# Attention scores drained two PSUM banks at a time, and every value product in three rounded passes

## The chip, the cores and the metric

The kernel runs on one core of one Trainium2 chip. The metric is the device time of one execution in microseconds (us); of several runs the median counts. A core has a matrix engine (TensorE, PE in the profile; its weight loads are PEld), a vector engine (VectorE, DVE), ScalarE (ACT), GpSimd (POOL) and SyncE (SP), which issues most of the DMAs here. Matrix results land in PSUM, which has 8 banks of 512 fp32 columns; VectorE and ScalarE read them from there.

## The reference, cut to what matters

The reference is one layer of a diffusion backbone over 2048 latent tokens with 256 context tokens, width 1024, all in fp32. One input projection feeds two head groups: gated linear attention, and differential softmax attention with 4 heads. Only the second is touched here:

```
s = einsum('bhqcd,bhkcd->bhcqk', q, k_all) * DIFF_DH ** -0.5     # c: two maps per head
p = softmax(s, axis=-1)
a = p[:, :, 0] - lam * p[:, :, 1]
o = einsum('bhqk,bhkd->bhqd', a, v_all)
```

There are 2304 keys (context and latent). `o` is normalised per head, joined with the other group's output, and goes through the output projection `w_out` with a gated residual; a SwiGLU feed-forward follows.

## The kernel before, in words

Precision comes from splitting. `split(hi, lo, src)` (L88) makes a rounded copy `hi` of a tile on ScalarE (L89, type float32r) and the rest `lo = src - hi` on VectorE (L86). `mm3` (L91 to L94) then makes a product in three passes, hi*hi, lo*hi and hi*lo (L92, L93, L94). A product of two fp32 tiles takes one call and no split; the profile shows it as two records.

The kernel runs in stages: input projections (stage 1), linear attention (stage 2), differential attention (stage 3), output projection (stage 4), feed-forward (stages 5 and 6). In stages 1 to 4 what TensorE does follows the order of the program; the other engines' instructions are put in order by the framework, by priority.

In stage 3, work is cut into 16 blocks, 4 heads times 4 groups of 4 query tiles (128 queries each). Two streams are interleaved on TensorE:

- `score_stream`. For each query tile and each map c there is a row of scores, 128 x 2304, made in five chunks (`CH`: four of 512 columns, one of 256). A chunk is two matmuls into one PSUM bank (L775, L776), with queries split into `qh` and `ql`. VectorE then drains it (L777): it copies the bank into the row `p` in SBUF and writes the chunk's maximum into `mx`. After the fifth chunk the maximum over `mx` is taken (L781) and ScalarE replaces the row by its exponential with the row's sum (L783). `combine` then scales the second map's row on VectorE (L807, two halves of 1152 columns) and GpSimd adds it to the first (L83). The chunks' banks come from the pool `s3ps` with `NS` = 4 buffers of one bank.
- `av_stream`. For each block and each of 18 key tiles it transposes four 128x128 pieces of `p` into one bank (L820), copies them out, and two steps later multiplies them with the value tile into the bank `o`. For key tiles whose number modulo 6 is in `VFP` = (0, 3), the copy is `at` (ScalarE, L823) and the product is one fp32 product (L843). For the others the copy is the split pair `ah` (ScalarE, L89) and `al` (VectorE, L86), and the product is `mm3`. At the end of a block `ot` and `on` are copied out and stored (L848 to L864).

There are 128 rows of scores, 640 chunks, and 288 value products, of which 96 in fp32. The PSUM use of stage 3 is 4 banks for chunks, 3 for transposes, 1 for `o`. Value tiles come from DRAM, written in stage 1 (`proj`): whole for the fp32 ones (`vf`), as `vh` and `vl` for the others; `load_v` fetches them in groups of six.

In stage 4, `prep(lt)` makes the operand of one token tile: it loads the attention's output into `mx`, squares it on ScalarE with `mh` as scratch (L985), scales it (L995), transposes `mx` in two halves (L1002) and splits it into `mh` and `ml`. `main(lt)` multiplies with the split `w_out` rows `wo`, in the orders `ORD0` and `ORD1`. The raw rows of `w_out` are loaded into staging tiles `wr` that are borrowed from other pools, and split during the last block of stage 3. Pools of a stage are stacked on one another in the order in which they are entered, so a tile of stage 4 lies over certain tiles of stage 3 and waits for just these to be released.

Of the kernel before, what the change touches and what calls it, by code (L numbers as in the profile page):

```python
# [11 lines left out]
F32 = mybir.dt.float32  # L12
F32R = mybir.dt.float32r
AF = mybir.ActivationFunctionType
ALU = mybir.AluOpType
AX = mybir.AxisListType
PSUM = bass.MemoryType.PSUM
DRAM = bass.MemoryType.DRAM

P = 128  # L20
# [12 lines left out]
NS, NTB, NO = 4, 3, 1  # L33
# [6 lines left out]
CD, LAG, LOOK = 4, 12, 2  # L40
MS = {mybir.EngineType.PE}
BKL = (3, 6, 9, 12)
PB, VFP = 6, (0, 3)
CSPLIT = ((2, 0, 1152), (2, 1152, 2304))
WPOOL = (0,)
VF = tuple(t for t in range(NK // P) if t % 6 in VFP)
VH = tuple(t for t in range(NK // P) if t not in VF)
# [4 lines left out]
def dit_block(ctx: ExitStack, tc: tile.TileContext, x, c, cx, c_ctx, w_mod, b_mod, norm1_g, w_in, gate_up,  # L52
              gate_bias, gla_g, qn_g, kn_g, lam_q, lam_k, diff_g, w_out, norm2_g, w_fi, w_fo,
              cosf, sinf, lmask, out, dbg=None):
    nc = tc.nc
    V, S, T, G = nc.vector, nc.scalar, nc.tensor, nc.gpsimd
# [13 lines left out]
    def dtile(name, shape, dt=F32):  # L70
        return dram.tile(list(shape), dt, name=name, tag=name)
# [16 lines left out]
    def split(hi, lo, src):  # L88
        return S.activation(hi, src, AF.Copy), sub(lo, src, f(hi))  # L89

    def mm3(ps, a, b, start, stop, **how):  # L91
# [36 lines left out]
    su_d = [(dtile(f"sf{t}", [64, 512]), dtile(f"ub{t}", [64, 512])) for t in range(NT)]  # L128
    q_d = [dtile(f"q{u}", [P, 4, SEQ], F32R) for u in "hl"]
    k_d = [dtile(f"k{u}", [P, 4, NK], F32R) for u in "hl"]  # L130
    v_d = {"f": dtile("vf", [P, len(VF), 512]), "h": dtile("vh", [P, len(VH), 512], F32R),
           "l": dtile("vl", [P, len(VH), 512], F32R)}
    md_d = [[dtile(f"md{h}_{t}", [P, P]) for t in range(NT)] for h in range(4)]
    x1_d = [dtile(f"x1_{t}", [P, D]) for t in range(NT)]
# [37 lines left out]
    with ExitStack() as st:  # L172
# [3 lines left out]
        st1 = st.enter_context(ExitStack())  # L176
# [12 lines left out]
        for t in range(2):  # L189
            xt = wk.tile([P, D], F32, name="xt", tag="xt")  # L190
# [514 lines left out]
    with ExitStack() as st:  # L705
        sm = st.enter_context(tc.tile_pool(name="s3m", bufs=6, reuse_waits="tile"))
# [4 lines left out]
        qp = st.enter_context(tc.tile_pool(name="s3q", bufs=2, reuse_waits="tile"))  # L711
        kp_ = st.enter_context(tc.tile_pool(name="s3k", bufs=3, reuse_waits="tile"))
        pb = st.enter_context(tc.tile_pool(name="s3pb", bufs=PB, reuse_waits="tile"))
        ps_s = st.enter_context(tc.tile_pool(name="s3ps", bufs=NS, space=PSUM, reuse_waits="tile"))
        ps_t = st.enter_context(tc.tile_pool(name="s3pt", bufs=NTB, space=PSUM, reuse_waits="tile"))
        ps_o = st.enter_context(tc.tile_pool(name="s3po", bufs=NO, space=PSUM, reuse_waits="tile"))
        NKT = NK // P
        CH = [(0, 512), (512, 512), (1024, 512), (1536, 512), (2048, 256)]
# [42 lines left out]
        def score_stream():  # L761
            later, ring = [], iter(range(64))
            for bi, (h, qb, i0, nq) in enumerate(blocks):
                as_[bi] = []
                for i in range(i0, i0 + nq):
                    qd = qs_[h, qb, i // 2]
                    qc = slice(i % 2 * P, (i % 2 + 1) * P)
                    pr = [(pa if next(ring) % (4 + PB) < 4 else pb).tile([P, NK], F32, name="p0", tag="p0"), sp.tile([P, NK], F32, name="p1", tag="p1")]
                    as_[bi].append(pr[0])
                    ls = []  # L770
                    for c_ in range(2):
                        mx = sm.tile([P, 5], F32, name="mx", tag="mx")
                        for j, (o0, n) in enumerate(CH):
                            ps = ps_s.tile([P, 512], F32, name="s", tag="s")
                            T.matmul(ps[:, 0:n], qd[0][c_][:, qc], ks_[h, c_][:, o0:o0 + n], start=True, stop=False)  # L775
                            T.matmul(ps[:, 0:n], qd[1][c_][:, qc], ks_[h, c_][:, o0:o0 + n], start=False, stop=True)  # L776
                            V.tensor_scalar(out=pr[c_][:, o0:o0 + n], in0=ps[:, 0:n], scalar1=1.0, scalar2=-3.0e38,  # L777
                                            op0=ALU.mult, op1=ALU.max, accum_out=mx[:, j:j + 1])
                            if j == len(CH) - 1:
                                nm = sm.tile([P, 1], F32, name="nm", tag="nm")  # L780
                                V.tensor_reduce(out=nm, in_=mx, axis=AX.X, op=ALU.max, negate=True)  # L781
                                l = l0all[:, qb * 4 + i, h:h + 1] if c_ == 0 else sm.tile([P, 1], F32, name="l1", tag="l1")
                                S.activation(pr[c_], pr[c_], AF.Exp, bias=nm, accum_out=l)  # L783
                                ls.append(l)
                                if c_ == 1:
                                    later.append([CD, combine(pr, ls, bi == len(blocks) - 1 and i >= i0 + nq - 2)])
                            for e in list(later):
                                e[0] -= 1
                                if e[0] < 0:
                                    e[1]()  # L790
                                    later.remove(e)
                            yield
            for e in later:
                e[1]()
# [72 lines left out]
        due, n = [], 0  # L867
# [26 lines left out]
    with ExitStack() as st:  # L894
# [16 lines left out]
        st1 = st.enter_context(ExitStack())  # L911
        xlp = rsk.enter_context(tc.tile_pool(name="s4xl", bufs=1, side="right", reuse_waits="tile"))
        gp = st1.enter_context(tc.tile_pool(name="s4gt", bufs=1, reuse_waits="tile"))
        htp = st1.enter_context(tc.tile_pool(name="s4ht", bufs=2, reuse_waits="tile"))
        wp = st1.enter_context(tc.tile_pool(name="s4w", bufs=1, reuse_waits="tile"))
        ph = st1.enter_context(tc.tile_pool(name="s4h", bufs=2, reuse_waits="tile"))
        ps_gm = st1.enter_context(tc.tile_pool(name="s4gm", bufs=1, space=PSUM, reuse_waits="tile"))
        ps_tp = st1.enter_context(tc.tile_pool(name="s4tp", bufs=3, space=PSUM, reuse_waits="tile"))
        ps_mm = st1.enter_context(tc.tile_pool(name="s4mm", bufs=4, space=PSUM, reuse_waits="tile"))
# [2 lines left out]
        xp = st1e.enter_context(tc.tile_pool(name="s4x", bufs=4, side="right", reuse_waits="tile"))  # L922
        xnp = st1e.enter_context(tc.tile_pool(name="s4n", bufs=2, side="right", reuse_waits="tile"))
        pp = st1e.enter_context(tc.tile_pool(name="s4p", bufs=2, reuse_waits="tile"))
# [4 lines left out]
        state = {}  # L929
        wo = {k: tuple(wp.tile([P, D], F32R, name=f"wo{u}_{k}") for u in "hl") for k in ORD1}  # L930
        for n, k in enumerate(ORD0):
            pool, tag = {3: (xnp, "xn"), 2: (xnp, "xn"), 1: (ph, "mh"), 0: (ph, "ml")}.get(k, (xp, "xt"))
            w = pool.tile([P, D], F32, name="wr", tag=tag)
            load(w, w_out[0, k * P:(k + 1) * P, :])
            with tc.high_priority(offset=tc.cur_priority - marks[3 + 2 * n]):
                split(*wo[k], w)
# [316 lines left out]
        with tc.manual_schedule(engines=MS):  # L1253
# [6 lines left out]
            for m, (n, i) in enumerate(flat):  # L1260
# [13 lines left out]
                ps = product(n, i)  # L1274
# [27 lines left out]
        with tc.manual_schedule(engines=MS):  # L1302
            for n, (dd, lt) in enumerate(pairs):
                js = slice(dd * 512, (dd + 1) * 512)
                ps = [ps6.tile([P, 512], F32, name="o", tag="o") for _ in range(2)]
# [73 lines left out]
```

## Time and profile before

| | |
|---|---|
| median of 3 runs | 3092.88 us (3092.88 to 3094.99) |
| the profiled execution: its time, its span | 3094.64 us, 3092.9 us |
| busy: PE, PEld, DVE | 3016.1 us (98%), 2483.7 us (80%), 2203.8 us (71%) |
| busy: ACT, POOL | 1423.5 us (46%), 463.8 us (15%) |
| granted TensorE clock, mean | 0.992 |
| the score drains (L777) | 640, 382.3 us busy |
| fp32 value products (L843) | 192 records, 922.2 to 1514.1 us |

Busy time is the union of an engine's instructions. Matmuls overlap in the pipeline, so a record is longer than the step from one matmul to the next; the same holds, less strongly, for VectorE. How long an instruction holds its engine is read from the timeline, as the step from its start to the next start where nothing was waited for. Shares over the whole span mix stages with different limits; the stretches of stage 3 are looked at by themselves.

### The profile page before, as it was taken

To read this page: it belongs to the slowest core of one execution; us is meant where nothing else is said; L and a number is where in the kernel's file an instruction comes from. 1 tells how busy PE (TensorE), PEld (TensorE's weight loads), DVE (VectorE), ACT (ScalarE), POOL (GpSimd) and SP (SyncE) were. 2 spreads that over 40 slices of the span, in tenths; PEclk is the share of its full clock that TensorE was granted. 3 is DMA by queue.
4 is the path that set the end of the run, shared out by engine and by line. 5 is a ranking of instruction groups with operands and counts; after the bars stand their busy time and mean duration, and the time that the engine had idled before them with its cause. 6 is when DMAs were issued, how large, how long until landed. Compare 5 with 4: busy or idle time off the path is not lost.

```text
span 3092.9 us, 41887 instructions
## 1 busy us (share of the span) xinstructions
PE 3016.1 (98%) x15124; PEld 2483.7 (80%) x15124; DVE 2203.8 (71%) x4788; ACT 1423.5 (46%) x2259; POOL 463.8 (15%) x290
## 2 busy tenths in 40 slices
PE   7999999999989999999999999999999999999999
PEld 4888888888867777777787788888788888888887
DVE  6887768888889999999787776666766666324232
ACT  5333366666657777777644433333433333113111
POOL 2111100000036555555111000000000000000000
PEclk9999999999999999999999999999999999999999
DMA  8876511121151313121445442222322225445342
GB/s 312 280 237 224 192 66 63 66 93 65 49 154 34 91 34 93 35 76 35 143 164 163 158 136 82 82 85 69 88 82 86 82 86 179 149 136 180 130 135 90
DMA packets 319121, 363.46 MB, mean 118 GB/s; under 512 B 25409, under 2 KB 256258, under 8 KB 312258
## 3 DMA queue, kind: packets, MB, share of 16 engines
q1 hardware_dynamic: 316322, 351.35, 36.2%
q0 software_dynamic: 2304, 8.39, 0.7%
q8 instruction: 119, 1.95, 0.3%
q10 hardware_dynamic: 288, 1.05, 0.1%
q14 instruction: 88, 0.72, 0.1%
HBM read 249.96 MB, written 110.76 MB: 117 GB/s over the span
## 4 chain that ended last, share of the span: by engine, by line
PE 63%; DVE 4%; issue 2%; DMA 1%; ACT 1%; POOL 1%; DVEq 0%; SPq 0%; ACTq 0%; POOLq 0%
PE p L93 9%; PE p L92 9%; PE p L94 9%; PE o L93 6%; PE o L94 6%; PE o L92 6%; PE s L775 4%; PE s L776 4%; PE t L820 4%; PE o L843 3%; PE mm L92 1%; PE mm L93 1%; PE mm L94 1%; POOL p L83 0%; DMA wo<-in_w_ffn_out 0%
## 5 line engine op out<-in xcount | busy, mean ns | idle before, releaser
L83 POOL TENSOR_TENSOR p<-p,p 128x1152 f32<-128x1152 f32 x124 | 354.8, 2882 | 283.5 <-DVE p L807 175.8
L777 DVE TENSOR_SCALAR_CACHE_REDUCE p<-s 128x512 f32<-128x512 f32 (+1 forms) x640 | 382.3, 632 | 13.2 <-PE s L776 9.2
L92 PE MATMUL mm<-wh,hh 128*128 128x512 f32 (+2 forms) x976 | 378.7, 388 | 0.0
L94 PE MATMUL mm<-wh,hl 128*128 128x512 f32 (+2 forms) x976 | 355.0, 364 | 1.1 <-DVE hl L86 1.1
L93 PE MATMUL mm<-wl,hh 128*128 128x512 f32 (+2 forms) x976 | 353.8, 363 | 0.0
L783 ACT ACTIVATE p<-p,nm 128x2304 f32<-128x2304 f32 x128 | 283.8, 2217 | 44.5 <-DVE nm L781 44.5
L775 PE MATMUL s<-k,qh 128*128 128x512 f32 (+1 forms) x640 | 276.4, 436 | 7.7 <-DVE p L777 6.9
L83 DVE TENSOR_TENSOR e<-p,e 128x512 f32<-128x512 f32 x220 | 152.1, 691 | 161.1 <-PE p L94 161.1
L92 PE MATMUL o<-wot,ah 128*128 128x512 f32 x682 | 265.4, 389 | 1.1 <-ACT wot L89 1.1
L93 PE MATMUL o<-wot,ah 128*128 128x512 f32 x682 | 265.4, 389 | 0.2 <-DVE wot L86 0.2
L94 PE MATMUL o<-wot,al 128*128 128x512 f32 x682 | 265.3, 389 | 0.0
L89 ACT ACTIVATE wh<-wi 128x512 fp32r<-128x512 f32 x172 | 108.4, 631 | 293.4 <-PE p L93 228.4
L776 PE MATMUL s<-k,ql 128*128 128x512 f32 (+1 forms) x640 | 235.6, 375 | 1.3 <-DMA ql<-ql 1.3
L89 ACT ACTIVATE ah<-ar 128x1408 fp32r<-128x1408 f32 x62 | 82.6, 1374 | 318.0 <-PE o L93 314.4
L94 PEld LDWEIGHTS mm<-wh,hl 128*128 128x128 f32 x976 | 184.8, 189 | 31.2 <-DVE hl L86 1.5
L92 PEld LDWEIGHTS mm<-wh,hh 128*128 128x128 f32 x976 | 185.9, 190 | 22.9 <-issue 0.7
L93 PEld LDWEIGHTS mm<-wl,hh 128*128 128x128 f32 x976 | 186.1, 191 | 21.4 <-issue 0.5
L86 DVE TENSOR_TENSOR al<-ar,ah 128x1408 fp32r<-128x1408 f32 x62 | 98.3, 1622 | 134.1 <-ACT ah L89 134.1
L89 ACT ACTIVATE wh<-s 128x512 fp32r<-128x512 f32 x128 | 80.9, 632 | 221.9 <-PE p L93 208.5
L820 PE MATMUL t<-ident,p 128*128 128x128 f32 x1152 | 173.3, 273 | 0.8 <-POOL p L83 0.8
L820 PEld LDWEIGHTS t<-ident,p 128*128 128x128 f32 x1152 | 141.5, 141 | 35.3 <-issue 3.7
L775 PEld LDWEIGHTS s<-k,qh 128*128 128x128 f32 x640 | 122.5, 191 | 57.9 <-DVE p L777 15.8
(317 smaller groups left out, 7135.9 us busy)
## 6 DMA issues: line engine op xcount, KB each, us to landing
ar<-act SPq DMA_DIRECT2D x64, 704.0 KB, 5.9
wi<-in_w_ffn_in SPq DMA_DIRECT2D x86, 512.0 KB, 5.0
act<-e SPq DMA_DIRECT2D x88, 256.0 KB, 2.6
wm<-in_w_mod SPq DMA_DIRECT2D x32, 512.0 KB, 5.0
xt<-in_x SPq DMA_DIRECT2D x30, 512.0 KB, 4.7
wr<-in_w_in SPq DMA_DIRECT2D x12, 1024.0 KB, 7.8
hdh<-hh SPq DMA_DIRECT2D x9, 1024.0 KB, 4.8
hdl<-hl SPq DMA_DIRECT2D x9, 1024.0 KB, 6.6
```

Of the source, the lines that this page charges most:

```text
L83: (eng or V).tensor_tensor(out=o, in0=a, in1=b, op=ALU.add)
L86: return (eng or V).tensor_tensor(out=o, in0=a, in1=b, op=ALU.subtract)
L89: return S.activation(hi, src, AF.Copy), sub(lo, src, f(hi))
L92: T.matmul(ps, a[0], b[0], start=start, stop=False, **how)
L93: T.matmul(ps, a[0], b[1], start=False, stop=False, **how)
L94: T.matmul(ps, a[1], b[0], start=False, stop=stop, **how)
L775: T.matmul(ps[:, 0:n], qd[0][c_][:, qc], ks_[h, c_][:, o0:o0 + n], start=True, stop=False)
L776: T.matmul(ps[:, 0:n], qd[1][c_][:, qc], ks_[h, c_][:, o0:o0 + n], start=False, stop=True)
L777: V.tensor_scalar(out=pr[c_][:, o0:o0 + n], in0=ps[:, 0:n], scalar1=1.0, scalar2=-3.0e38, op0=ALU.mult, op1=ALU.max, accum_out=mx[:, j:j + 1])
L783: S.activation(pr[c_], pr[c_], AF.Exp, bias=nm, accum_out=l)
L820: T.transpose(pt[:, i, :], as_[bi][i][:, kt * P:(kt + 1) * P], ident)
L843: T.matmul(po[:, 0:nq, :], v[0], at[0], start=kt == 0, stop=kt == NKT - 1)
```

## The change

Three things change.

- `VFP` becomes empty: all 288 value products are made by `mm3` from split operands. The DRAM tensor `vf` goes, `vh` and `vl` hold all 18 key tiles, and the value tiles in SBUF take 12 tiles of 128 columns per group of six keys instead of 10.
- Chunks of scores are made in pairs: a buffer of the pool `s3ps` is two banks, there are `NS // 2` = 2 of them, and one drain copies both banks (1024 columns). The fifth chunk has a buffer of its own and its own drain of 256 columns. `mx` has 3 columns instead of 5.
- In stage 4 the pool `ph` (tiles `mh`, `ml`) is entered before `htp` and `wp` instead of behind them, and the raw rows 1 and 0 of `w_out` are staged in `pp` (tag `mx`) instead of `ph`.

```
-PB, VFP = 6, (0, 3)
+PB, VFP = 6, ()
...
-    v_d = {"f": dtile("vf", [P, len(VF), 512]), "h": dtile("vh", [P, len(VH), 512], F32R),
+    v_d = {"h": dtile("vh", [P, len(VH), 512], F32R),
...
-        ps_s = st.enter_context(tc.tile_pool(name="s3ps", bufs=NS, space=PSUM, reuse_waits="tile"))
+        ps_s = st.enter_context(tc.tile_pool(name="s3ps", bufs=NS // 2, space=PSUM, reuse_waits="tile"))
...
-                        mx = sm.tile([P, 5], F32, name="mx", tag="mx")
+                        mx = sm.tile([P, 3], F32, name="mx", tag="mx")
                         for j, (o0, n) in enumerate(CH):
-                            ps = ps_s.tile([P, 512], F32, name="s", tag="s")
+
+                            if j % 2 == 0:
+                                ps2 = ps_s.tile([P, 2, 512], F32, name="s", tag="s")
+                            ps = ps2[:, j % 2]
                             T.matmul(ps[:, 0:n], qd[0][c_][:, qc], ks_[h, c_][:, o0:o0 + n], start=True, stop=False)
                             T.matmul(ps[:, 0:n], qd[1][c_][:, qc], ks_[h, c_][:, o0:o0 + n], start=False, stop=True)
-                            V.tensor_scalar(out=pr[c_][:, o0:o0 + n], in0=ps[:, 0:n], scalar1=1.0, scalar2=-3.0e38,
-                                            op0=ALU.mult, op1=ALU.max, accum_out=mx[:, j:j + 1])
+                            if j % 2 or j == len(CH) - 1:
+                                a0 = j // 2 * 1024
+                                V.tensor_scalar(out=pr[c_][:, a0:o0 + n], in0=ps2.rearrange("p b n -> p (b n)")[:, 0:o0 + n - a0],
+                                                scalar1=1.0, scalar2=-3.0e38, op0=ALU.mult, op1=ALU.max,
+                                                accum_out=mx[:, j // 2:j // 2 + 1])
...
         gp = st1.enter_context(tc.tile_pool(name="s4gt", bufs=1, reuse_waits="tile"))
+        ph = st1.enter_context(tc.tile_pool(name="s4h", bufs=2, reuse_waits="tile"))
         htp = st1.enter_context(tc.tile_pool(name="s4ht", bufs=2, reuse_waits="tile"))
         wp = st1.enter_context(tc.tile_pool(name="s4w", bufs=1, reuse_waits="tile"))
-        ph = st1.enter_context(tc.tile_pool(name="s4h", bufs=2, reuse_waits="tile"))
...
-            pool, tag = {3: (xnp, "xn"), 2: (xnp, "xn"), 1: (ph, "mh"), 0: (ph, "ml")}.get(k, (xp, "xt"))
+            pool, tag = {3: (xnp, "xn"), 2: (xnp, "xn"), 1: (pp, "mx"), 0: (pp, "mx")}.get(k, (xp, "xt"))
```

## Rows read from the trace of the kernel before

**Rows 1.** Busy time by stretch: us, engines' busy us (instructions), clock, DMA share, GB/s.

```profile
core 0: us, PE busy (x) PEld busy (x) DVE busy (x) ACT busy (x) POOL busy (x), PEclk, DMA share, GB/s
200.00:400.00 200.00, 196.38 (x972) 163.58 (x971) 151.34 (x298) 70.24 (x124) 28.81 (x55) 0.98 0.60 199
876.00:1486.00 610.00, 600.42 (x3110) 471.90 (x3109) 587.61 (x1837) 448.02 (x551) 354.84 (x124) 0.99 0.24 65
890.00:950.00 60.00, 52.72 (x227) 38.64 (x226) 54.09 (x181) 37.76 (x41) 38.09 (x14) 0.89 0.28 86
1486.00:1516.00 30.00, 28.20 (x152) 20.46 (x151) 24.44 (x39) 28.07 (x61) 1.29 (x1) 1.00 0.61 184
```

**Rows 2.** Waits of PE, 950 to 1486 us: total us, times, longest.

```profile
PE o L93 <- DVE al L86: 0.3, 1, 0.3
```

**Rows 3.** Groups by shape on DVE, 876 to 1486 us: busy, mean ns, idle before.

```profile
L777 DVE TENSOR_SCALAR_CACHE_REDUCE p<-s 128x512 f32<-128x512 f32 x512 | 336.8, 687 | 13.2 <-PE s L776 9.2 <-POOL p L83 4.1
L86 DVE TENSOR_TENSOR al<-t,ah 128x512 fp32r<-128x512 f32 x177 | 121.6, 687 | 2.9 <-ACT ah L89 2.9
```

**Rows 4.** Waits of DVE, 876 to 1486 us.

```profile
DVE p L777 <- PE s L776: 9.2, 32, 1.3
DVE r L799 <- ACT p L783: 7.1, 28, 0.3
DVE p L777 <- POOL p L83: 4.1, 3, 1.4
DVE al L86 <- ACT ah L89: 2.9, 14, 0.2
```

**Rows 5.** Timeline of PE: start us, length us, instruction.

```profile
1306.43 0.60 PE L820 MATMUL t<-ident,p 128*128 128x128 f32 x4
...
1307.95 0.39 PE L776 MATMUL s<-k,ql 128*128 128x512 f32 x1
...
1310.67 0.39 PE L776 MATMUL s<-k,ql 128*128 128x512 f32 x1
1310.90 0.60 PE L820 MATMUL t<-ident,p 128*128 128x128 f32 x4
...
1312.04 0.40 PE L775 MATMUL s<-k,qh 128*128 128x512 f32 x1
```

**Rows 6.** Groups by shape on PE, 876 to 1486 us.

```profile
L843 PE MATMUL o<-at,vf 128*128 128x512 f32 x178 | 91.1, 594 | 0.0
```

**Rows 7.** Timeline of DVE.

```profile
1300.12 0.69 DVE L86 TENSOR_TENSOR al<-t,ah 128x512 fp32r<-128x512 f32 x1
1300.72 0.42 DVE L777 TENSOR_SCALAR_CACHE_REDUCE p<-s 128x256 f32<-128x256 f32 x1
1301.06 0.09 DVE L777 DVE_READ_ACCUMULATOR p<-s 128x1 f32 x1
1301.06 0.69 DVE L777 TENSOR_SCALAR_CACHE_REDUCE p<-s 128x512 f32<-128x512 f32 x1
1301.67 0.09 DVE L777 DVE_READ_ACCUMULATOR p<-s 128x1 f32 x1
...
1305.74 1.54 DVE L807 TENSOR_SCALAR p<-p,cf 128x1152 f32<-128x1152 f32 x2
```

**Rows 8.** Timeline of ACT and PE around the change of stage.

```profile
1504.78 0.35 ACT L985 ACTIVATE mh<-mx 128x128 fp32r<-128x128 f32 x1
...
1511.11 0.40 ACT L995 ACTIVATE mx<-mx,rs 128x128 f32<-128x128 f32 x1
...
1515.73 0.39 PE L94 MATMUL o<-ah,vl 128*128 128x512 f32 x1
...
1516.85 0.61 PE L860 MATMUL t<-ident,ot 128*128 128x128 f32 x4
1517.30 0.60 PE L1002 MATMUL tp<-ident,mx 128*128 128x128 f32 x4
1522.04 1.09 PE L1002 MATMUL tp<-ident,mx 128*128 128x128 f32 x4 [4.15 <-DVE mx L80]
1522.78 0.78 PE L92 MATMUL mm<-woh,mh 128*128 128x512 f32 x1
```

## The prediction, made before the changed kernel was run

> **What bounds the kernel now.** I read the busy times by stretch first. The change touches the attention stage, and in it above all the stretch in which scores are made, 876 to 1486 us [rows 1]: the matrix engine is busy 600.4 of 610 us, the vector engine 587.6, idle 22.4. A busy matrix engine may hide waits, since matmuls overlap, so I went to what it waits for: from 950 us on, with the start-up over, one wait of 0.3 us is left [rows 2]. So the matrix engine is the bound, and the vector engine stands 3.7% behind it. Of a second engine so close the reader wants to know what it does: the groups by shape [rows 3] say score drains and the subtractions that make `al`, besides the scaling of p1. Its idle time is four small waits [rows 4]: 9.2 us for score matmuls, 7.1 for the exponential, 4.1 for GpSimd, 2.9 for `ah`.
>
> The reader is to see two engines nearly in balance: a change that takes work from one and gives work to the other can win no more than the other has idle.
>
> **The change part by part.**
>
> *Value products: what the matrix engine saves.* 6 of 18 key tiles in each of 16 blocks, 96 products, go from one fp32 product to three rounded passes. Two stretches that are alike but for the product [rows 5]: with fp32, from the transposes at 1306.43 to the second score matmul at 1307.95 it is 1.52 us; less 0.23 for the first score matmul (the step between neighbours that do not wait, 1310.67 to 1310.90) that is 1.29. With three passes, from 1310.90 to 1312.04, it is 1.14. Saved: 0.15 us each. The score stretch holds 178 fp32 records [rows 6], two to a product, so 89 products: 13.4 us. The 7 in the tail: 1.1 us.
>
> *The same products on the vector engine: the work it gains.* A product in three passes needs `al`, one subtraction over 128x512 from PSUM. ScalarE's copy is there either way (`at` becomes `ah`, same shape), so ScalarE gets nothing new. The `al` at 1300.12 is followed by the next instruction at 1300.72 [rows 7]: 0.60 us. 89 of them: 53.4 us.
>
> *Pair drains: the work it loses.* Five drains of a row become three. A 512 drain holds the engine 0.61 us (1301.06 to 1301.67), a 256 drain 0.34 (1300.72 to 1301.06) [rows 7]. The accumulator read behind a drain starts together with the next instruction, so it costs nothing that could be saved. 256 columns more cost 0.27 us; a 1024 drain, which no row shows, should hold the engine 0.61 + 2 x 0.27 = 1.15, and a pair saves 2 x 0.61 - 1.15 = 0.07. Bounds: the slope alone, without any fixed part, gives 4 x 0.27 = 1.08 and saves 0.14; two drains' worth, 1.22, saves nothing. I take 0.07, from the same instruction's own two sizes. 128 rows of scores with two pairs each: 256 x 0.07 = 17.9 us (0 to 36).
>
> A page of the Trainium skill bears on this: Perfetto Trace Analysis, section Optimizing Scalar/DVE Operations, puts the fixed price of a vector instruction on PSUM at about 125 ns and advises larger operations where that engine is saturated. By it the merges would give back 32 us, as an estimate, and the sum below would be 14 us lower; the rows show a fixed part of about 0.07 us (0.61 - 2 x 0.27).
>
> *Sum for the score stretch.* Vector engine: 587.6 + 53.4 - 17.9 = 623.1 us. Matrix engine: the stretch that it sets falls to 610 - 13.4 = 597. So the vector engine becomes the bound, and the stretch can't be shorter than 623, 13 us more than now. To this comes its idle time. The waits for the exponential, GpSimd and `ah` (14.1 us) have nothing to do with the matrix engine's load and stay; of the 9.2 for score matmuls I keep 4, since that engine now has 26 us to spare but fewer buffers to run ahead into. 623.1 + 18 = 641: +31 us. Idle time can be 0 (+13) or the 10% of the start-up stretch 890 to 950, where the vector engine was busy 54.1 of 60 us [rows 1] (+82).
>
> *Buffers.* Four one-bank buffers become two of two banks; no row shows that state. Before, a bank is held for filling (2 x 0.23) and drain (0.61), 1.07 us, and comes round every 4 x 610 / 640 = 3.8 us: 2.7 us to spare. After, a buffer is held for 4 x 0.23 + 1.15 = 2.07 us and comes round every 2 x 641 / 384 = 3.3: 1.3 us to spare. A value step with its transposes takes 1.14 us of the matrix engine, the two scalings of p1 some 1.5 of the vector engine (1.54 for both in [rows 7]). One of these in a turn is hidden, both are not. That is the first rival.
>
> *Tail, 1486 to 1516.* 7 more subtractions, 4.2 us, against 5.6 us idle of the vector engine [rows 1]; the matrix engine has 1.1 us less. Taken as 0 (-1 to +4).
>
> *Change of stage.* `ph` moves ahead of `htp` and `wp`, so `mh` now begins where `gt1` ends. Adding up the tile sizes in the code from the pools' common base, that is at 69,632 bytes; the attention's `al` lies, with the larger value tiles, at 64,448 to 72,640, and `ot` behind it up to 74,688. So the first `mh` waits until the last `ot` is read; before, it lay over p0 buffers, and its squares ran at 1504.78 [rows 8]. `ot` is read by the transposes at 1516.85, so the squares start about 12.6 us later, near 1517.4. From the first square to the last scaling of `mx` it was 1504.78 to 1511.5, 6.7 us, between other work of ScalarE: so at the latest 1524.1, and then the transposes that ran at 1517.30. But the matrix engine stood until 1522.04 anyway for the other half of `mx`, and its first output product came at 1522.78 [rows 8]; only what goes past that counts. I take +2 us (0 to 5). The last two weight rows are staged in `pp`, where the first `mx` then waits for the split of weight row 1; `mx` is used long after it lands, so 0, and if that cover fails it falls within the same 5 us.
>
> *Stage 1.* 6 tiles get a subtraction (0.60 each) and one store more. The vector engine is busy 151 of 200 us there [rows 1]: 0, and 3.6 us without that cover. Value loads on SyncE's queue become 2 instead of 3 for each group, with the DMA engines 24% busy in the score stretch: 0.
>
> **Total.** 31 + 0 + 2 = +33 us on the profiled execution's own 3094.6: 3128. The median of the runs lies 1.8 us below that execution, so 3126.
>
> **The rivals.**
> - *Two pair buffers are too few* (0.15). The engines wait for each other in the turns in which a value step and the scalings of p1 meet. For: the spare time of a turn halves. Against: the vector engine mostly has an `al` to do meanwhile. With 7% idle, between the 3.7% of now and the 10% of the start-up, 623.1 / 0.93 = 670: +60 + 2, 3155. It decides from about 4% idle. The Trainium skill's page Perfetto Trace Analysis, sections Identifying the Most-Contended Engine and Optimizing Scalar/DVE Operations, speaks for this rival: repeating gaps can mean too little PSUM, and smaller instructions may let work finish sooner; no run shows the two-buffer state yet.
> - *The vector engine runs without a gap* (0.15): +13 and less with a cheaper pair, 3095 + 13 - 4: about 3104.
> - *Faster: merging gives back more than the subtractions take* (0.06). The matrix engine stays the bound and its 14.5 us come through: 3078. The vector engine would have to fit 597 us with the 14 of idle time that stay: (587.6 + 53.4 + 14 - 597) / 256 = 0.23 us saved by a pair, a 1024 drain of 0.99, below even the slope alone (1.08).
> - *Level* (0.06): with 18 us idle a pair must save 0.19; with none, 0.12.
>
> The forecast itself has 0.58.
>
> **How the numbers follow.** The point is 3126. Below 3104 lie the faster and level cases and half of the gap-free one; above 3152 some of the buffer case: together 2 in 10. Within 0.2% (6 us) of before counts as the same, about what a measurement of this kernel can tell. Faster 0.06, same 0.06, slower 0.88.
>
> **What would show it.** Right: in the score stretch the vector engine over 96% busy and the stretch near 640 us; the matrix engine waiting for drains of `p` some 20 to 40 us; a 1024 drain that holds the engine 1.15; 288 `al` of 0.69. Wrong: a matrix engine still full in a shorter stretch (a drain below its slope), or a vector engine under 95% busy with waits for score matmuls (buffers). The change of stage is right if the squares into `mh` come after the last attention transposes, and the first output product 7 to 12 us after the last value product instead of 7.

## The result, and the profile after

The kernel after takes 3201.25 us (median of 4 runs, 3199.41 to 3202.46), the kernel before 3093.93 in the same session. The ratio is 1.0345, 95% interval 1.0327 to 1.0363: slower by 107 us, where the forecast was 33 and its range ended at 3152.

Of the 104.8 us between the two profiled executions (3094.64 and 3199.41) the score stretch has nearly all. The last score drain ends at 1585.2 us instead of 1485.3, 99.9 us later. From there to the last value product it is 33 us instead of 31, and the first output product follows that 9.4 us later instead of 7.1.

The window of the score stretch of after, with the columns of [rows 1]; it now ends at 1586:

```profile
876.00:1586.00 710.00, 621.98 (x3185) 480.53 (x3184) 629.57 (x1413) 446.10 (x550) 354.06 (x124) 0.99 0.21 57
```

The vector engine is busy 629.6 us, against 623.1 in the forecast. But the stretch has 710, so it is idle for 80.4, against 18. The matrix engine is no longer full either: 622 of 710. Neither engine bounds the stretch by itself.

The waits of the vector engine in the stretch, which answer to [rows 4], and those of the matrix engine from 950 us on, which answer to [rows 2]:

```profile
DVE p L782 <- PE s L779: 35.3, 55, 1.7
DVE al L86 <- ACT ah L89: 23.8, 29, 0.8
DVE r L805 <- ACT p L789: 20.6, 43, 1.0
```

```profile
PE s L778 <- DVE p L782: 68.0, 58, 1.3
```

Before, the same three waits were 9.2, 2.9 and 7.1 us, and the matrix engine had no wait for a drain there. Now each waits for the other. The chain of work that ended last, in the page of after, goes back and forth between them (before, it had 63% PE and 4% DVE):

```profile
PE 52%; DVE 17%; ACT 4%; issue 3%; DMA 0%; SPq 0%; DVEq 0%; ACTq 0%
```

Where the matrix engine's waits stand, from its groups by shape in the stretch (after the second bar: idle time before them, and its releaser):

```profile
L778 PE MATMUL s<-k,qh 128*128 128x512 f32 x509 | 217.8, 428 | 80.8 <-DVE p L782 78.8
...
L778 PE MATMUL s<-k,qh 128*128 128x256 f32 x128 | 40.1, 314 | 7.0 <-DVE p L782 6.1
```

Before the 256-column chunk, the fifth of a row, there is hardly a wait; they stand before chunks of 512. Counted over the records of the trace between 950 and 1585 us, a wait taken as what a step is longer than between neighbours that do not wait, about 76 of 90 us stand in 56 places, each time before the first chunk of a row. They do not all follow the scalings of p1: half of them end 4.5 to 5.1 us behind the start of a pair of scalings, the other half 10 to 11 us behind it. One of the first kind on the timeline, first the matrix engine, then the vector engine, then ScalarE:

```profile
1297.97 0.40 PE L94 MATMUL o<-ah,vl 128*128 128x512 f32 x1
1298.37 0.38 PE L778 MATMUL s<-k,qh 128*128 128x256 f32 x1
1298.59 0.28 PE L779 MATMUL s<-k,ql 128*128 128x256 f32 x1
1300.11 0.50 PE L778 MATMUL s<-k,qh 128*128 128x512 f32 x1 [1.24 <-DVE p L782]
...
1300.68 0.60 PE L826 MATMUL t<-ident,p 128*128 128x128 f32 x4
```

```profile
1297.09 1.22 DVE L782 TENSOR_SCALAR_CACHE_REDUCE p<-s 128x1024 f32<-128x1024 f32 x1
1298.23 0.09 DVE L782 DVE_READ_ACCUMULATOR p<-s 128x1 f32 x1
1298.23 0.69 DVE L86 TENSOR_TENSOR al<-t,ah 128x512 fp32r<-128x512 f32 x1
1298.83 1.22 DVE L782 TENSOR_SCALAR_CACHE_REDUCE p<-s 128x1024 f32<-128x1024 f32 x1
1299.97 0.09 DVE L782 DVE_READ_ACCUMULATOR p<-s 128x1 f32 x1
```

```profile
1301.37 0.60 ACT L89 ACTIVATE ah<-t 128x512 fp32r<-128x512 f32 x1 [1.97 <-PE t L826]
```

The drain at 1297.09 is of a row's first pair, that at 1298.83 of its second. The fifth chunk takes the buffer that the first drain freed and fills it with two short matmuls. The next row's first chunk needs the other buffer; its drain begins at 1298.83, behind an `al`, and ends at 1299.97. The matrix engine stands until 1300.11. It takes its instructions in the order of the program, so the transposes (1300.68) and value products behind this matmul stand too, though they need no score buffer, and ScalarE waits 1.97 us for these transposes before its next `ah`.

The durations were as forecast, and the scalings of p1 as before. The drain at 1297.09 holds the vector engine until 1298.23, 1.14 us (forecast 1.15); the `al` at 1298.23 holds it 0.60. The groups of the vector engine, beside [rows 3]:

```profile
L782 DVE TENSOR_SCALAR_CACHE_REDUCE p<-s 128x1024 f32<-128x1024 f32 x256 | 311.1, 1217 | 35.5 <-PE s L779 35.3
L86 DVE TENSOR_TENSOR al<-t,ah 128x512 fp32r<-128x512 f32 x265 | 180.9, 685 | 23.8 <-ACT ah L89 23.8
L813 DVE TENSOR_SCALAR p<-p,cf 128x1152 f32<-128x1152 f32 x124 | 95.6, 813 | 0.0
```

The change of stage, beside [rows 8], first the matrix engine, then ScalarE. The squares into `mh` (1622.22) now come after the last attention transposes (1618.89), and the transposes of `mx` wait for them:

```profile
1617.81 0.40 PE L94 MATMUL o<-ah,vl 128*128 128x512 f32 x1
...
1618.89 0.66 PE L866 MATMUL t<-ident,ot 128*128 128x128 f32 x4
1625.04 2.20 PE L1008 MATMUL tp<-ident,mx 128*128 128x128 f32 x8 [5.49 <-ACT mx L1001]
1627.17 0.80 PE L92 MATMUL mm<-woh,mh 128*128 128x512 f32 x1
```

```profile
1622.22 0.29 ACT L991 ACTIVATE mh<-mx 128x128 fp32r<-128x128 f32 x1
```

### The profile page after: what moved, and what is told of

Read it like the earlier page. It is cut to its first block, busy times and chain, and to the rows that moved or that the text cites. A ratio compares the mean times of both kernels' runs of the same rounds, so it can differ in the third digit from the quotient of the medians.

```text
span 3197.4 us, 41645 instructions
## 1 busy us (share of the span) xinstructions
PE 3039.9 (95%) x15220; PEld 2497.3 (78%) x15220; DVE 2260.3 (71%) x4378; ACT 1423.7 (45%) x2259; POOL 464.0 (15%) x290
## 3 DMA queue, kind: packets, MB, share of 16 engines
q0 software_dynamic: 2304, 8.39, 0.7%
q8 instruction: 120, 1.97, 0.3%
## 4 chain that ended last, share of the span: by engine, by line
PE 52%; DVE 17%; ACT 4%; issue 3%; DMA 0%; SPq 0%; DVEq 0%; ACTq 0%
PE p L93 8%; PE p L92 8%; PE p L94 8%; DVE p L782 6%; PE o L93 6%; PE o L94 5%; PE o L92 5%; DVE p L813 3%; DVE al L86 2%; ACT p L789 2%; PE s L778 2%; PE mm L92 1%; PE t L826 1%; PE mm L93 1%; PE s L779 1%
## 5 line engine op out<-in xcount | busy, mean ns | idle before, releaser
L782 DVE TENSOR_SCALAR_CACHE_REDUCE p<-s 128x1024 f32<-128x1024 f32 (+1 forms) x384 | 361.5, 950 | 35.5 <-PE s L779 35.3
L778 PE MATMUL s<-k,qh 128*128 128x512 f32 (+1 forms) x640 | 259.2, 405 | 88.3 <-DVE p L782 84.9
L89 ACT ACTIVATE ah<-t 128x512 fp32r<-128x512 f32 x288 | 165.2, 590 | 185.8 <-PE t L826 185.5
L86 DVE TENSOR_TENSOR al<-t,ah 128x512 fp32r<-128x512 f32 x288 | 196.2, 685 | 24.8 <-ACT ah L89 24.5
```

The source lines that it names most:

```text
L86: return (eng or V).tensor_tensor(out=o, in0=a, in1=b, op=ALU.subtract)
L782: V.tensor_scalar(out=pr[c_][:, a0:o0 + n], in0=ps2.rearrange("p b n -> p (b n)")[:, 0:o0 + n - a0], scalar1=1.0, scalar2=-3.0e38, op0=ALU ...
```

## The experiments

Each kernel is the one before or after with the edit shown. Where no interval stands, the time is of one run, beside 3092 to 3097 us of the kernel before on the same chip.

**Three passes with one-bank drains.** From after, the score drains as before:

```
-        ps_s = st.enter_context(tc.tile_pool(name="s3ps", bufs=NS // 2, space=PSUM, reuse_waits="tile"))
+        ps_s = st.enter_context(tc.tile_pool(name="s3ps", bufs=NS, space=PSUM, reuse_waits="tile"))
...
+                            ps = ps_s.tile([P, 512], F32, name="s", tag="s")
...
+                            V.tensor_scalar(out=pr[c_][:, o0:o0 + n], in0=ps[:, 0:n], scalar1=1.0, scalar2=-3.0e38,
+                                            op0=ALU.mult, op1=ALU.max, accum_out=mx[:, j:j + 1])
```

> The changed kernel with the drains of before: four one-bank score buffers, five drains a row; every value product still in three passes. Theory 'buffers' (the 80 us of idle time of the vector engine in the score stretch come from two pair buffers for three chunks' worth of turns a row): idle time falls back to about 20 us though the vector engine's work grows by 18; score stretch 587.6 + 53.4 + 20 = 661 us, whole kernel about 3150, some 50 us faster than the changed kernel. Rival 'subtractions' (a vector engine with 53 us more work, in the order that the framework gave it, loses that time by itself, whatever the buffers): idle time stays near 80, stretch about 720, kernel about 3215.

3130.3 us, 33 more than before. Its score stretch, and the waits of the vector engine and of the matrix engine there:

```profile
876.00:1516.00 640.00, 621.44 (x3202) 482.98 (x3201) 633.23 (x1927) 448.24 (x551) 354.92 (x124) 0.99 0.24 64
```

```profile
DVE p L777 <- POOL p L83: 3.0, 3, 1.4
DVE p L777 <- PE s L776: 2.1, 3, 1.3
...
PE s L775 <- DVE p L777: 6.8, 11, 1.3
```

The vector engine is busy 633 of 640 us: here it is the bound, by the mechanism of the forecast. The other 71 us of the result belong to the pairs.

**Pair drains alone.** From before: the second of the three things that change, the chunks made in pairs, with `VFP = (0, 3)` and the pools of before.

> The kernel before with the pair drains alone: two buffers of two banks, three drains a row; fp32 value products and the output projection's pools as before. Theory 'buffers': the matrix engine, full before, waits for the drains as in the changed kernel (85 us there); score stretch 650 to 690 us, kernel 3135 to 3175. Rival 'subtractions': the vector engine has 18 us less work and the matrix engine stays full: stretch 610, kernel 3090 to 3096.

3214.2 us, 117 more than before, and 13 more than the whole change; the theory's 3135 to 3175 was too low. The vector engine had less to do than in after (612 us busy in a stretch of 726), and still the matrix engine waits for it. The stretch, then the waits:

```profile
876.00:1602.00 726.00, 639.45 (x3104) 475.27 (x3104) 612.00 (x1323) 452.72 (x551) 347.87 (x124) 0.98 0.20 55
...
PE s L778 <- DVE p L782: 82.9, 92, 2.4
...
DVE p L782 <- PE s L779: 58.7, 74, 1.7
```

So the pairs do the harm without any `al` added. The 13 us that the three passes give back on top of them (15 without the 2 us of the pools, below) are close to what the forecast put down for the matrix engine (13.4 + 1.1), but the granted clock differs too, 0.98 in this stretch against 0.99 in that of after.

**Pair buffers, two drains.** From after:

```
-                            if j % 2 or j == len(CH) - 1:
...
+                            V.tensor_scalar(out=pr[c_][:, o0:o0 + n], in0=ps[:, 0:n], scalar1=1.0, scalar2=-3.0e38,
+                                            op0=ALU.mult, op1=ALU.max, accum_out=mx[:, j:j + 1])
```

> The changed kernel with its two buffers of two banks, but each bank drained by an instruction of its own (five drains a row); a buffer is free when both are drained. Theory 'buffers' in the form that the size and number of the buffers decide: time as the changed kernel's, within 15 us (3185 to 3215), with about 18 us more work on the vector engine and the same waits for drains. Its other form, that the one long instruction decides (it can't start before both banks are filled, and releases both only at its end): idle time falls by half or more, kernel 3150 to 3175.

3432.2 us, a miss that does not test what it was meant to. First the matrix engine, then the vector engine:

```profile
1294.29 0.50 PE L778 MATMUL s<-k,qh 128*128 128x512 f32 x1 [2.03 <-DVE p L780]
1294.63 0.40 PE L779 MATMUL s<-k,ql 128*128 128x512 f32 x1
1294.86 0.28 PE L778 MATMUL s<-k,qh 128*128 128x256 f32 x1
...
1293.54 0.68 DVE L780 TENSOR_SCALAR_CACHE_REDUCE p<-s 128x512 f32<-128x512 f32 x1
```

The matmul at 1294.29 stands two before the 256-column chunk, so it fills the second bank of a pair, and it waits for the drain of the first bank of the same pair. With two drains, fill and drain of one buffer take turns; the matrix engine waits 239 us for drains in all. Not all of the time is this: the granted clock is lower here (0.97 over the run), and 33 scalings of p1 last longer than 1 us, by 50 us in all; the kernel with three equal turns below shows why.

**The fifth chunk in a bank of its own.** From after; the bank is taken from the transposes:

```
-NS, NTB, NO = 4, 3, 1
+NS, NTB, NO = 4, 2, 1
+        ps_5 = st.enter_context(tc.tile_pool(name="s3p5", bufs=1, space=PSUM, reuse_waits="tile"))
...
+                            if j == len(CH) - 1:
+                                ps2 = ps_5.tile([P, 1, 512], F32, name="s5", tag="s5")
```

> The changed kernel with a one-bank buffer of its own for the fifth chunk of a row (256 columns), taken from the transposes, which keep two banks of three. Theory 'buffers', narrowed to the third turn of a row: the two pair buffers then serve two pairs a row, the next row's first pair no longer waits for this row's second pair; waits of the matrix engine for drains fall from 85 us to under 30, stretch 645 to 665, kernel 3135 to 3155. Rival 'subtractions': no change but for the lost transpose bank, 3195 or more.

3138.7 us, 63 less than after. Its control, with `NTB` = 2 alone:

> The changed kernel with two banks for the transposes instead of three and nothing else (the bank is left unused): the control for the run in which the fifth chunk has its bank. If a transpose bank costs nothing, 3198 to 3204 as the changed kernel; if it costs, up to 3220, and the gain of the fifth chunk's own bank was larger than the 62 us seen.

3219.8 us. The missing bank of transposes costs 19 us, so the bank for the fifth chunk gives back 81. The waits of the matrix engine with the fifth chunk alone:

```profile
PE t L869 <- DVE al L86: 17.1, 14, 1.2
PE s L781 <- DVE p L785: 15.7, 22, 3.5
```

Its waits for drains fall from 85 us to 16; the first row is the missing transpose bank. The drains of 1024 columns are still there, so with a third buffer the long drain does little harm.

**The pools alone.** From before: the third of the three things that change.

> The kernel before with the third change alone: the pool of mh and ml entered first, the last two weight rows staged in pp. In the changed kernel 9.4 us lay between the last value product and the first output product, 7.1 before. Expected: +2 to +3 us (ratio 1.0007 to 1.001), from that gap alone. Rival (the cover holds in the kernel before, where the attention's tiles lie 3 KB lower): 0 to 1 us.

3095.9 against 3093.7 us, ratio 1.0009 (1.0001 to 1.0018): 2 us, as forecast.

**Value steps behind the second and fifth chunk.** From after:

```
-            due += [n + LAG + kt * 10 * blk[3] / NKT for kt in range(NKT)]
+            due += [n + o for o in (11, 14, 16, 19, 21, 22, 24, 26, 29, 31, 34, 36, 39, 41, 42, 44, 46, 49)]
```

> The changed kernel with another order of work on the matrix engine alone: 16 of a block's 18 value steps stand behind the second and the fifth chunk of a row instead of evenly spread (the other two behind the third), so that a step always lies between a fifth chunk and the next row's first. Theory 'third turn' (the fifth chunk fills its buffer in 0.23 us, so the next row's first pair comes to the buffer of the second pair before that is drained; an even spread puts a value step in between only in part of the rows): waits of the matrix engine for drains fall from 85 us to about half, kernel 3140 to 3170. Rival (too little buffering in whatever order, the waits move to other places): 3190 to 3215.

3212.3 us. The idea that the order of the matrix engine's work makes the wait fell: its waits for drains are 80.0 us in 78 places (84.9 in 80 in after); by the records they only moved, about 44 us before a row's first chunk and 42 before its fifth.

**Fifth chunk alone, 3 of 18 key tiles in fp32.** The kernel with the fifth chunk in a bank of its own, with the DRAM tensor `vf` again, and

```
-PB, VFP = 6, ()
+PB, VFP = 6, (0,)
```

> Pair drains with the fifth chunk in its own bank (transposes have two), and 3 of 18 key tiles in fp32 instead of 6 or none: the vector engine would need 587.6 + 26.7 - 17.9 = 596 us in the score stretch, the matrix engine 610 - 6.7 = 603. If the waits are gone with the third turn: about 3090, some 5 us faster than before. If they stay as with no fp32 product (a stretch some 20 us longer than the vector engine's work): 3100 to 3115.

3143.8 us (3 rounds; ratio to before 1.0161, 1.0146 to 1.0177), 5 us more than without, and outside both expectations. The vector engine is busy 595 us instead of 617 and yet nothing is won: less work for it does not shorten the stretch when pairs are drained, even with the fifth chunk apart.

**Three equal turns.** From after: is it the short turn of the fifth chunk, or are two buffers too few in any case?

```
-        CH = [(0, 512), (512, 512), (1024, 512), (1536, 512), (2048, 256)]
+        CH = [(0, 512), (512, 256), (768, 512), (1280, 256), (1536, 512), (2048, 256)]
...
-                                a0 = j // 2 * 1024
+                                a0 = j // 2 * 768
```

The counts by which value steps and loads are placed go from 10, 20 and 160 chunks to 12, 24 and 192. The second kernel also has `VFP` = (0,).

> The kernel after, but a row of scores is cut into three equal turns of 768 columns (chunks of 512 and 256 in each two-bank buffer) instead of turns of 1024, 1024 and 256. Buffers, drains per row, columns and value products stay. Theory: it is the short turn of the fifth chunk that hurts; it takes a whole buffer for 0.23 us of matrix work, so that the next row's first pair finds the other buffer's 1.14 us drain still running. Three equal turns with drains of about 0.88 us take that away: the score stretch falls from 710 us to 645 to 670, the matrix engine's waits for drains from 85 us to under 45, and the time to 3135 to 3160 us, near the 3130 of one-bank drains. Rival: two buffers are too few however the row is cut; then the waits only spread over the three turns, the stretch stays at 690 or more and the time at 3180 to 3200 us.

> As the kernel with three equal turns, but 3 of the 18 key tiles again as fp32 products: 26.7 us less for the vector engine in the score stretch, 6.7 us more for the matrix engine. If three equal turns leave the vector engine as the bound, this gains 10 to 25 us on them. If the two engines still take turns, as in the kernel with the fifth chunk in its own bank, it loses 0 to 10 us.

3285.8 and 3234.8 us, both outside what was expected. The first answer is no, but both runs show something else. The vector engine and GpSimd in the kernel with three equal turns, then the matrix engine, then two windows of 10 us:

```profile
1390.61 0.82 DVE L813 TENSOR_SCALAR p<-p,cf 128x1152 f32<-128x1152 f32 x1
1391.35 0.68 DVE L86 TENSOR_TENSOR al<-t,ah 128x512 fp32r<-128x512 f32 x1
1391.95 2.89 DVE L813 TENSOR_SCALAR p<-p,cf 128x1152 f32<-128x1152 f32 x1
...
1391.60 2.63 POOL L83 TENSOR_TENSOR p<-p,p 128x1152 f32<-128x1152 f32 x1 [4.07 <-DVE p L813]
```

```profile
1396.37 0.80 PE L778 MATMUL s<-k,qh 128*128 128x512 f32 x1 [3.50 <-DVE p L782]
...
1397.81 0.63 PE L778 MATMUL s<-k,qh 128*128 128x512 f32 x1
1398.24 0.63 PE L779 MATMUL s<-k,ql 128*128 128x512 f32 x1
```

```profile
1380.00:1390.00 10.00, 9.63 (x59) 8.01 (x58) 9.16 (x20) 7.36 (x11) 5.73 (x2) 1.00 0.24 68
1390.00:1400.00 10.00, 6.50 (x29) 5.24 (x29) 8.75 (x16) 3.97 (x6) 5.26 (x2) 0.74 0.05 14
```

An `al` came between the two scalings of a row, so GpSimd had begun to add the first half (1391.60) when the second scaling came up (1391.95); this one lasts 2.89 us instead of 0.82, to 0.6 us past the end of the add. Over the trace, what the scalings take beyond 0.82 us each is 60 us here and 32 with three tiles in fp32 (23 in pairs alone), against nothing in before and after, where the two scalings follow one another and the add begins behind the second. Of the 62 pairs of scalings here, 29 have another instruction between them, and just these 29 second scalings are the long ones. The matrix engine stands 3.5 us, and behind that, between 1396.3 and 1399.5, its granted clock is 0.50, the lower of its two levels, 1.2 GHz: the 512-column step is 0.43 us (1397.81 to 1398.24) instead of 0.23.

**Two one-bank buffers.** The kernel with one-bank drains, and

```
-NS, NTB, NO = 4, 3, 1
+NS, NTB, NO = 2, 3, 1
```

> The kernel with one-bank drains and all value products in three passes, but with two buffers of one bank instead of four: the number of buffers of the kernel after, with the short drain (0.61 us). Theory (the number of turns that the matrix engine can run ahead decides): both engines wait for each other as in the kernel after, the matrix engine waits for drains 60 us or more, and the time is 3180 to 3300 us instead of 3130. Rival (the length of the drain decides, not the number of buffers): 3130 to 3160 us, since a drain of 0.61 us hardly outlasts the 0.46 us of the next chunk's matmuls.

3209.3 us: 79 more than with four such buffers, and 8 more than the kernel after. The waits for drains add up as in after, but in more places (89.0 us in 138; in after 84.9 us in 80):

```profile
PE s L775 <- DVE p L777: 89.0, 138, 2.1
...
DVE p L777 <- PE s L776: 30.4, 57, 1.3
```

With drains of 0.61 us and two buffers the loss is there; with drains of 0.61 us and four it is not, and with drains of 1.14 us and a third buffer (the fifth chunk apart) most of it is gone. So the number of buffers decides more than the length of the drain. The run is not after with shorter drains, though: it has two banks for scores and not four, and by the records from 950 us on 61 of some 95 us of waits stand before the third chunk of a row, 2.2 us behind the start of the scalings of p1, where in after they stand before the first.

**One scaling, one add.** To take the collision away, a row is scaled in one instruction and added in one:

```
-CSPLIT = ((2, 0, 1152), (2, 1152, 2304))
+CSPLIT = ((2, 0, 2304),)
```

on the kernel with three equal turns, on pairs alone, and on after as the control.

> The kernel with three equal turns of 768 columns, but the second map's row is scaled on the vector engine in one instruction of 2304 columns instead of two of 1152, and added by GpSimd in one. In the kernel with three equal turns the second scaling often ran while GpSimd already added the first half, and then took up to 2.9 us instead of 0.82; one scaling cannot meet the add of its own row. Theory one (two buffers are too few however the row is cut): the 60 us of longer scalings go, and with them the matrix engine's longest waits and its lower granted clock, but the waits for drains stay over 60 us and the time at 3185 to 3225 us. Theory two (it is the fifth chunk's short turn): without the collisions the equal turns show their worth, 3135 to 3165 us.

> The kernel with pair drains alone (fp32 products kept), with the same single scaling and single add of a row. In pairs alone 19 scalings took over 1.0 us, 25 us more than 128 of 0.82. If that is why pairs alone cost more than the whole change, the time falls from 3214 by 20 to 35 us, to 3180 to 3195; if the longer scalings lie in idle time, it stays within 8 us of 3214.

> Control: the kernel after with the single scaling and add. There only 4 scalings were longer than 1.0 us (2.4 us in all), so nothing is to be won: 3190 to 3212 us. If the single scaling of 1.5 us in one piece makes new waits, it is slower than that, and the two runs beside it are to be read against it.

3182.9, 3210.3 and 3194.8 us. (The four longer scalings in the expectation of the control are instructions of 1.41 us that scale and add in one, and four of the 19 in pairs alone are such too.) The equal turns lose 103 us by it and stand 12 under their control, just below the band of theory one and 18 us above that of theory two. The waits in the score stretch of the equal turns with one scaling:

```profile
PE s L778 <- DVE p L782: 40.1, 55, 2.6
...
DVE p L782 <- PE s L779: 55.3, 69, 5.1
```

The matrix engine's waits for drains are halved, not gone: the short turn is a part of the cause, worth some 12 us by one run each, and two buffers remain too few. Pairs alone hardly gain: the vector engine has less to do (581 us in a stretch of 718 instead of 612 in 726), the time falls by 4 us. The longer scalings there lay in idle time; my expectation of 20 to 35 us fell. What is left to explain why pairs alone cost more than the whole change are the matrix engine's longer fp32 products and the lower granted clock (0.98 in the score stretch here too); which of them it is, no run shows.

**One scaling in the kernel before.**

> The kernel before, with the second map's row scaled in one instruction and added in one. The kernel after became 5 to 6 us faster by this edit. If that came from less vector work (two instructions of 1.55 us in all become one of about 1.42), the kernel before, which the matrix engine bounds, gains 0 to 2 us: 3091 to 3094 us. If the single add of twice the length reaches the end of a block later and the transposes wait for it, it loses 2 to 8 us.

3106.0 against 3092.2 us (5 rounds; ratio 1.0044, 1.0030 to 1.0057): slower, by more than I allowed. The score stretch ends 10.5 us later, at 1495.8. The largest of the matrix engine's waits in it (0.8 us, once, in before):

```profile
PE t L820 <- POOL p L83: 9.8, 15, 3.5
```

The transposes wait for the longer add, in 15 places for 16 blocks. No version tried beats the kernel before.

## Why the prediction was wrong

*Which engine becomes the bound, and the three passes.* The mechanism was right where it could be seen by itself: with four one-bank buffers the vector engine is 99% busy, and the time is up 33 us. That this is also the forecast's number is chance in part: without the pairs its terms give 587.6 + 53.4 + 18 = 659 us of stretch, and it was 640, with 633 of work and 7 of idle time. The sum's pieces hold in after too: `al` 0.60, the 1024 drain 1.14, the engine's work 629.6 us against 623.1.

*Tail and change of stage.* Right: the tail is 2.2 us longer (0, with -1 to +4), the gap before the first output product 2.3 us (2, with 0 to 5), and the pools alone cost 2 us.

*The idle time: the step that failed.* The sum for the score stretch kept 18 us of idle time for the vector engine, 4 of it for score matmuls, and said that the other 14.1 "have nothing to do with the matrix engine's load and stay". Measured: 80.4, of which 35.3 for score matmuls, 23.8 for `ah` and 20.6 for the exponential. This term alone, 62 us too small, makes up most of the miss of 75; the vector engine's work has 6.5 of the rest. What was wrong in it:
- The Buffers paragraph added fill and drain as if a drain began when its last matmul ended. It begins later, since the vector engine has an `al`, a scaling or another drain before it, and a value step can fall into the filling. Counted over the records, from a buffer's first score matmul until its drain lets the engine go, a bank was held 2.22 us on average before (950 to 1486 us), where the paragraph has 1.07, and a pair buffer 3.20 us after (950 to 1585, all turns), where it has 2.07. Against the paragraph's round of 3.3 us that leaves 0.1 us to spare, not 1.3; the trace of before showed the longer hold already.
- The paragraph also worked with an average turn. Three turns of 1024, 1024 and 256 columns go over two buffers, and when the fifth chunk has one of them, the matrix engine comes to the other 0.5 us later (in the place shown). Turns of equal size give some 12 us back.
- The larger part is the number of turns that the matrix engine can run ahead: one instead of three. Two buffers of one bank lose 79 us against four, with short drains and unchanged instructions (though in other places and with half the banks); a third buffer beside the two pairs gives 81 us back.
- "The vector engine mostly has an `al` to do meanwhile" left out that the `al` comes from the same queue. A matmul that waits for a buffer holds up the transposes behind it, so `ah` and the next `al` come late, and so does the row that the exponential waits for. Hence all three waits grew together, not the one for score matmuls alone; with four one-bank buffers, where the matrix engine's waits for drains are 6.8 us, the waits for `ah` and the exponential are nearly gone too (0.8 and 0.6 us).

The first rival, *two pair buffers are too few*, named the cause, and its sign in the profile was there (DVE 89% busy, with waits for score matmuls). The place that it named, where a value step and the scalings of p1 meet, covers half of the waits at most: the other half end 10 to 11 us behind the start of the scalings. It was given 0.15 and 7% idle; it is 11.3% (80.4 of 710). With that share the rival's own formula gives 623.1 / 0.887 = 702, +92 + 2 on 3093: 3187, within 14 us. The start-up stretch 890 to 950 had shown 10% idle with all four buffers [rows 1], and the prediction named it as the upper end (+82) but left it outside its range (+59).

A rule of the Trainium skill, Perfetto Trace Analysis, section Optimization Strategy (the prediction named another section of that page for it), says that gaps that repeat through a stretch can mean too little SBUF or PSUM for the next tile. The trace agrees: some 76 us in 56 like gaps, and more buffers removed them where less vector work did not.

Open is what the remaining loss of the equal turns with one scaling (53 us over the one-bank drains) is made of; the granted clock, 0.98 over the stretch, is 1.00 from 950 us to its end, so in the stretch the clock counts in the start-up alone. Whether the vector engine's order, an `al` or the scalings ahead of a drain that the matrix engine waits for, adds to the loss was not tried. Three buffers of two banks beside three banks for transposes and one for `o` do not fit into eight banks and were not tried.

## What to carry to other kernels

Merging two PSUM drains into one is paid with buffers: count how many turns the producer can run ahead before and after, and read from the trace how long a buffer is really held, with the time that its drain stands behind other work. Look at the turns one by one, unequal ones above all, since an average turn hides the place where two meet. Where the producer's queue also carries the consumer's other work, a wait for a buffer starves both, and the idle time of every kind grows, not only the wait that was asked about. Try the halved number of buffers with the old instructions first; it needs one constant, and here it cost 79 us where the pairs cost 71, though it waits in other places.

## What the runs showed of the hardware that was not expected

- A scaling from SBUF to SBUF on the vector engine that meets an add of GpSimd lasts until the add is over: up to 2.9 us for one of 0.82, 60 us over the kernel with three equal turns, while instructions that read PSUM kept their length: in after, the drain at 1297.09 and the `al` at 1298.23 ran beside two adds of GpSimd (from 1295.95, 5.70 us in all). The Trainium skill, SBUF — State Buffer, section Who interferes with whom, states that the two share a pair of ports, that an instruction such as `tensor_scalar` can enter a mode that takes this pair, and that whoever comes second is then blocked for the whole instruction; the trace agrees (the add ends at 1394.23, the scaling at 1394.84). What decides in these traces is whether another instruction falls between the two scalings, so an edit elsewhere can bring the collision in.
- One scaling of 2304 columns takes 1.42 us, two of 1152 back to back 1.55; the kernel before got 14 us slower with the shorter one, with 9.8 us of waits of transposes for the longer add.
